# A Strassen MLP whose first products take their weight block sums from VectorE, with the tiles moved to other byte offsets

## The chip, the cores and the metric

The kernel runs on one core of one Trainium2 chip. The time is device microseconds for one execution, the median of three runs.

## The reference

One layer of a decoder with 512 tokens of width 1024, everything in float32. Two mixers run side by side on the same normalised input (sliding-window attention and a gated convolution), their outputs are gated, added and projected, and an MLP with a squared ReLU follows:

```python
u = rms_norm(x, norm_mix_g)
proj = u @ w_in                       # q, k, v, two convolution inputs, two gates
attn = sliding_window_attention(...) @ w_attn_o
conv = conformer_conv(...)           # ends in a product with w_conv_out
merged = jax.nn.sigmoid(gate_attn) * attn + jax.nn.sigmoid(gate_conv) * conv
x = x + merged @ w_out
hmid = jnp.square(jax.nn.relu(rms_norm(x, norm_mlp_g) @ w_ff1))   # 1024 -> 4096
x = x + hmid @ w_ff2                                              # 4096 -> 1024
```

## The kernel before, in words

Each float32 matrix is split into a high and a low part, each in a rounded format that TensorE multiplies at full rate, and a product is three matmuls: high by high, high by low, low by high. ScalarE (ACT) casts the high part; VectorE (DVE), or GpSimd (POOL) in some places, subtracts it from the whole to get the low part.

The program is written as a list of events, `at(pos, fn, ...)`, that is sorted by position before anything is issued. One unit of position is roughly 1.4 us of TensorE work. Each engine runs its instructions in that order, and so do the DMA queues of SP (plain loads) and POOL (loads that add to what is in the buffer). So a late instruction holds all that stands behind it on its engine or queue.

The stages are: projections, attention and convolution up to 313 us; the attention output product `ps_wo` (313 to 362 us); the convolution output product `ps_wc` (362 to 407); the product with `w_out` and the second norm (position `W0`, 407 to 453); and the MLP (position `M0 = W0 + 32`, 453.6 to 782.9).

The MLP works on four parts of the hidden width, each of 1024. A part is two phases of 28 units: an even phase is the first product (FF1: 512 x 1024 by 1024 x 1024, with `w_ff1`), an odd phase the second (FF2, with `w_ff2`). A phase is a Winograd form of Strassen's scheme with one level: seven products of half-size blocks, 4 units each, instead of eight. They run in `ORDER`: 1, 7, 6, 2, 5, 4, 3 (in phase 0: 1, 2, 7, 6, 5, 4, 3). In FF1 the weights stand in TensorE and the normalised `x` (tiles `xE`, `xO`, `xS`) streams by in 256 columns; in FF2 the activations (`aE`, `aO`, `aS`) stand and the weights stream by in 512 columns.

Of a phase's weight blocks b11, b12, b21, b22 the products need: 1: b11; 5: b11 + b12; 7: b12 + b22; 6: b11 + b12 + b22; 4: all four; 2: b21; 3: b22. A sum lies in a raw buffer of 128 x 2048 floats (two halves, `h` = 0 and 1, of 512 KB). For each half `piece_hi` (L1105, ACT) casts it to `pieceh` and `piece_lo` (L1108, DVE) subtracts to `piecel`; there are four buffers of pieces, so piece n waits until product half n - 4 has been run. `products` issues the matmuls (L1133 in FF1, L1138 in FF2).

The sums are made by the transfers: `fetch` (L1090, SP) loads a block, and `fetch_add` (L1094, POOL) loads another block with an add into the same buffer, after the pieces have read it:

```python
    BUF = {1: 0, 5: 0, 7: 1, 6: 1, 4: 1, 2: 2, 3: 2}
                if prod == 1:
                    at(d, fetch_add, ph, 0, 0, 1, h)
                elif prod == 7:
                    at(d, fetch_add, ph, 1, 0, 0, h)
                elif prod == 6:
                    at(d, fetch_add, ph, 1, 1, 0, h)
```

There are three raw buffers (`raw_b`, `raw_q0`, `raw_q1`). So each of the eight phases moves 8 MB: four plain blocks and four added ones. The results of FF1's products are combined by `c_copy`, `c_add`, `relu`, `square_of`; `operands` then makes from them the sums and splits for FF2 (`op_sum`, `op_hi`, `op_lo`). FF2's results are added to the residual rows by `row_add` (L1143).

Every tile has a byte offset in a partition's memory. The pools behind the small pool `sm` begin 192 bytes beyond a multiple of 256, those before it (`wp`, `keep`) on a multiple.

Of the kernel before, what the change touches and what calls it, by code (L numbers as in the profile page):

```python
# [17 lines left out]
P = 128  # L18
# [34 lines left out]
def tile_hybrid_block(  # L53
# [34 lines left out]
    sm.tile([P, LEAD // 4], F32, name="even", bufs=1)  # L88
# [370 lines left out]
    def split_lo(u):  # L459
        ge.tensor_tensor(out=pieces[u][1], in0=piece_of(u), in1=pieces[u][0].bitcast(F32), op=ALU.subtract)  # L460
# [197 lines left out]
    last_of = {wout[2]: b + 6.5, wout[3]: b + 12.5}  # L658
# [353 lines left out]
    def wout_split(ch, m, eng):  # L1012
        ks, raw = slice(2 * m, 2 * m + 2), raws[ch][:, 2 * (m % 2):2 * (m % 2) + 2, :]
        se.copy(tl["wouth"][:, ks, :], raw)
        eng.tensor_tensor(out=tl["woutl"][:, ks, :], in0=raw, in1=tl["wouth"][:, ks, :].bitcast(F32),
                          op=ALU.subtract)
# [31 lines left out]
    for m, p in enumerate((1.5, 6, 9.5, 12)):  # L1048
        at(W0 + p, wout_split, wout_late[m // 2], m, ge)
    at(W0 + 8, lambda: se.activation(roots[:, 0:1], epsc, AF.Sqrt))  # L1050
    for t in range(NT):
        at(W0 + 16.1 + 0.6 * t, lambda t=t: residual(t, 0, tl["acc"][t]))
        at(W0 + 16.6 + 0.6 * t, residual_square, t, 0)
# [6 lines left out]
        for half in range(2):  # L1060
            late = (0.8, 0.2, 0, 0)[t]
# [16 lines left out]
    BUF = {1: 0, 5: 0, 7: 1, 6: 1, 4: 1, 2: 2, 3: 2}  # L1078
# [17 lines left out]
    def open_mlp():  # L1096
        for n in range(2):
            tl["raw"].append(wp.tile([P, 4, S], F32, name=f"raw_q{n}", tag="raw", bufs=2))

    def open_pieces():  # L1100
        for n in "hl":
            tl["p" + n] += [wp.tile([P, 2, S], F32R, name=f"piece{n}{i}", tag="w" + n) for i in range(3)]
# [277 lines left out]
```

## Time and profile before

| | before |
|---|---|
| median of 3 runs | 788.52 us (787.55 to 788.69) |
| profiled execution | 788.5 us, span 786.7 us |
| granted clock of TensorE, mean | 0.997 |
| moved by DMA | 113.21 MB |
| on POOL's queue (adding transfers) | 33.56 MB |
| DMA in the MLP | 0.63 to 0.93 of the engines' time in each phase |

In the profile, PE is TensorE, PEld its weight loads. A row of a group of instructions gives the line, engine, operation, output <- inputs, shape and count; then the busy time in us and the mean of one in ns; then the idle time of the engine just ahead of them and what ended most of it. A row of the chain gives the time, the duration in us, what it was, and how many instructions. A row of waits gives who waited for whom: us in total, times, longest. A `DMA` row is a transfer, `raw_q` and `raw_b` being the raw buffers. Rows of the timeline give start, duration, engine, line, operation, count, and in brackets the wait ahead of it.

### The profile page before, as it was taken

The numbers are of one execution on the slowest core, as the hardware profiler recorded it, in microseconds if no ns is written. First come the engines' busy times: TensorE is split into PE (matmuls) and PEld (weight loads), VectorE is DVE, ScalarE is ACT, GpSimd is POOL, SyncE is SP. The second block draws the span as 40 slices with busy tenths as digits, with TensorE's granted clock in tenths as the row PEclk, the third lists the DMA queues.
The fourth block names the chain that finished last, engine by engine and source line by source line (L and its number), as shares of the span: only waits on it lengthen the run. The fifth ranks groups of instructions, "written<-read, shape, count | busy, mean of one in ns | idle before, by whom it ended". The sixth has DMA issues, their size and how long they took to land.

```text
span 786.7 us, 11648 instructions
## 1 busy us (share of the span) xinstructions
PE 766.4 (97%) x4464; PEld 668.5 (85%) x4464; DVE 566.0 (72%) x888; ACT 438.6 (56%) x696; POOL 332.1 (42%) x253
## 2 busy tenths in 40 slices
PE   8999999999999999999999998899999999999998
PEld 7989989898888888788888898779997899789976
DVE  5467978898888878975433577694679558875785
ACT  5445457766576665455335466652766367535851
POOL 4444978958565655334357012213131313131310
PEclk9999999999999999999999999999999999999999
DMA  8351041214141132522337637989898999899982
GB/s 272 105 173 54 1 161 54 82 54 135 53 132 58 54 107 68 201 84 77 107 130 234 145 55 183 192 208 216 218 199 202 212 229 194 194 213 207 219 167 107
DMA packets 74029, 113.21 MB, mean 144 GB/s; under 512 B 4004, under 2 KB 36820, under 8 KB 73974
## 3 DMA queue, kind: packets, MB, share of 16 engines
q1 hardware_dynamic: 56566, 78.91, 30.7%
q0 software_dynamic: 17408, 33.56, 24.2%
q8 instruction: 35, 0.57, 0.3%
q14 instruction: 20, 0.16, 0.1%
HBM read 110.33 MB, written 2.12 MB: 143 GB/s over the span
## 4 chain that ended last, share of the span: by engine, by line
PE 59%; DMA 13%; issue 10%; DVE 8%; POOL 6%; ACT 3%; POOLq 0%; SPq 0%; ACTq 0%; DVEq 0%
DMA raw_q<-in_w_ff_dram 12%; DVE piecel L1108 4%; PE ps_x L1133 3%; POOL raw_b L1094 2%; POOL raw_q L1094 2%; PE ps_ta L492 2%; PE ps_wc L492 2%; PE ps_wc L493 2%; PE ps_wc L494 2%; PE ps_ta L494 2%; PE ps_wo L196 2%; PE ps_wo L198 2%; PE ps_ta L493 2%; PE ps_wo L197 2%; PE ps_g L492 2%
## 5 line engine op out<-in xcount | busy, mean ns | idle before, releaser
L1094 POOL DMA_DIRECT2D raw_q<-in_w_ff_dram x48 | 58.8, 1226 | 222.4 <-DMA raw_q<-in_w_ff_dram 139.9
L794 DVE SCALAR_TENSOR_TENSOR cv<-h,wcol,cv 128x512 f32<-128x512 f32 x208 | 147.5, 747 | 0.5
L1108 DVE TENSOR_TENSOR piecel<-raw_q,pieceh 128x1024 fp32r<-128x1024 f32 x80 | 97.1, 1221 | 57.0 <-ACT pieceh L1105 56.9
L1105 ACT CAST pieceh<-raw_q 128x1024 fp32r<-128x1024 f32 x80 | 82.6, 1048 | 70.9 <-DMA raw_q<-in_w_ff_dram 51.5
L1108 DVE TENSOR_TENSOR piecel<-raw_b,pieceh 128x1024 fp32r<-128x1024 f32 x32 | 41.2, 1291 | 29.0 <-ACT pieceh L1105 29.0
L1133 PE MATMUL ps_x<-xSh,pieceh 128*128 128x256 f32 x192 | 54.3, 283 | 2.5 <-ACT c L1152 2.2
L1133 PE MATMUL ps_x<-xSh,piecel 128*128 128x256 f32 x192 | 54.5, 284 | 1.4 <-DVE piecel L1108 1.3
L1133 PE MATMUL ps_x<-xSl,pieceh 128*128 128x256 f32 x192 | 54.1, 282 | 0.0
L1138 PE MATMUL ps_z<-piecel,aSh 128*128 128x512 f32 x96 | 38.4, 400 | 5.4 <-DVE piecel L1108 5.4
L1105 ACT CAST pieceh<-raw_b 128x1024 fp32r<-128x1024 f32 x32 | 33.2, 1046 | 11.6 <-PE ps_y L1138 10.1
L703 ACT ACTIVATE s<-s,negm 128x257 f32<-128x257 f32 (+1 forms) x64 | 30.4, 478 | 16.2 <-DVE negm L695 16.2
L1133 PEld LDWEIGHTS ps_x<-xSh,pieceh 128*128 128x128 f32 x192 | 36.8, 191 | 2.9 <-ACT c L1152 2.4
L1138 PE MATMUL ps_z<-pieceh,aSh 128*128 128x512 f32 x96 | 37.5, 391 | 1.7 <-ACT pieceh L1105 1.7
L1133 PEld LDWEIGHTS ps_x<-xSh,piecel 128*128 128x128 f32 x192 | 36.4, 190 | 2.2 <-DVE piecel L1108 2.2
L1138 PE MATMUL ps_z<-pieceh,aSl 128*128 128x512 f32 x96 | 37.5, 391 | 0.0
L786 POOL TENSOR_TENSOR side<-side,tap 128x512 f32<-128x512 f32 x24 | 31.1, 1297 | 13.6 <-ACT tap L785 13.6
L196 PE MATMUL ps_q<-wh_q,uTh 128*128 128x256 f32 x128 | 36.6, 286 | 0.0
L1133 PEld LDWEIGHTS ps_x<-xSl,pieceh 128*128 128x128 f32 x192 | 36.4, 189 | 0.0
L727 DVE TENSOR_TENSOR pTl<-ptp,pTh 128x512 fp32r<-128x512 f32 x28 | 19.3, 690 | 23.7 <-ACT pTh L723 23.6
L198 PE MATMUL ps_q<-wh_q,uTl 128*128 128x256 f32 x128 | 36.2, 283 | 0.0
L197 PE MATMUL ps_q<-wl_q,uTh 128*128 128x256 f32 x128 | 36.2, 282 | 0.0
L1094 POOL DMA_DIRECT2D raw_b<-in_w_ff_dram x16 | 19.6, 1242 | 32.9 <-DVE piecel L1108 25.5
(325 smaller groups left out, 2600.8 us busy)
## 6 DMA issues: line engine op xcount, KB each, us to landing
raw_q<-in_w_ff_dram SPq DMA_DIRECT2D x48, 512.0 KB, 6.3
raw_q<-in_w_ff_dram POOLq DMA_DIRECT2D x48, 512.0 KB, 7.7
raw_b<-in_w_ff_dram SPq DMA_DIRECT2D x16, 512.0 KB, 8.0
raw_b<-in_w_ff_dram POOLq DMA_DIRECT2D x16, 512.0 KB, 8.8
x<-in_x_dram SPq DMA_DIRECT2D x8, 512.0 KB, 4.6
raw_g<-in_w_in_dram SPq DMA_DIRECT2D x8, 512.0 KB, 4.5
raw_a<-in_w_in_dram SPq DMA_DIRECT2D x8, 512.0 KB, 3.5
raw_q<-in_w_in_dram SPq DMA_DIRECT2D x8, 512.0 KB, 5.2
```

What stands on the lines that cost most here:

```text
L196: pe.matmul(ps, ah, wh, start=first, stop=False)
L197: pe.matmul(ps, ah, wl, start=False, stop=False)
L198: pe.matmul(ps, al, wh, start=False, stop=last)
L492: pe.matmul(ps, wh[:, k, :], ah(k), start=(k == 0), stop=False)
L493: pe.matmul(ps, wh[:, k, :], al(k), start=False, stop=False)
L494: pe.matmul(ps, wl[:, k, :], ah(k), start=False, stop=(k == KD - 1))
L794: ve.scalar_tensor_tensor(out=cps[ct], in0=src, scalar=w, in1=cps[ct], op0=ALU.mult, op1=ALU.add)
L1094: ge.dma_start(tl["raw"][buf][:, ks, :], block(ph, i, j)[:, ks, :], accum_op=ALU.add)
L1105: se.copy(tl["ph"][n % 4], tl["raw"][buf][:, 2 * h:2 * h + 2, :])
L1108: ve.tensor_tensor(out=tl["pl"][n % 4], in0=tl["raw"][buf][:, 2 * h:2 * h + 2, :], in1=tl["ph"][n % 4].bitcast(F32), op=ALU.subtract)
L1133: pe.matmul(o, b[:, c, w], a[:, k, :], start=(first and c + q + i == 0), stop=(k == 3 and i == 2), skip_group_check=True)
L1138: pe.matmul(acc, a[:, k, w], b[:, c, :], start=(first and c + i == 0), stop=(k == 3 and i == 2), skip_group_check=True)
```

## The change

*Block sums.* In FF1 phases the four blocks are loaded plainly into four raw buffers (`block0` to `block3`, whose roles `homes` rotates), and `block_sum` on DVE makes the sums in place: q1 = b11 + b12, q3 = b12 + b22, q2 = b11 + b12 + b22, q4 = that + b21, each in two halves. In phase 0 the last of these is still an adding transfer. FF2 phases keep the adding transfers, with other buffers: the sum for product 7 is loaded and added during the FF1 phase before (earlier than it was), the blocks of the next FF1 phase are loaded during FF2. So FF1 phases move 4 MB instead of 8.

*Order.* Pieces for product 6 go 2.5 units earlier in FF1, those for product 7 0.95 to 1.05 units in FF2 (`s`); first activation operands `P1`, `P2` and the later `x` operands move by 0.5 to 3.6 units. Some subtractions (`split_lo` for the second `w_out` chunk, the four `wout_lo`) move from POOL to DVE. In the `w_out` stage the buffers of blocks and pieces are opened one by one.

*Places.* The tile `even` is 64 bytes longer, a tile `shift` of 192 bytes is put in, and the order of tiles in the `ff` pool is changed. Then the FF2 operands and all four piece buffers begin on multiples of 256 bytes; `xE`, `xO`, `xS` stay 192 beyond one.

The diff, cut to its core:

```diff
-    sm.tile([P, LEAD // 4], F32, name="even", bufs=1)
+    sm.tile([P, LEAD // 4 + 16], F32, name="even", bufs=1)
...
-        ge.tensor_tensor(out=pieces[u][1], in0=piece_of(u), in1=pieces[u][0].bitcast(F32), op=ALU.subtract)
+        eng = ve if u in wout_uses[2:] else ge
+        eng.tensor_tensor(out=pieces[u][1], in0=piece_of(u), in1=pieces[u][0].bitcast(F32), op=ALU.subtract)
...
-        tl["raw"] = [pool.tile([P, 4, S], F32, name="raw_b")]
+        tl["raw"] = [pool.tile([P, 4, S], F32, name=f"block{i}") for i in range(2)]
...
+        gmlp = tl["gmlp"] = pool.tile([P, D], F32, name="gmlp", tag="aEh")
+        tl["fsq"] = pool.tile([P, 2, S], F32, name="fsq", tag="aEl")
+        pool.tile([P, 48], F32, name="shift")
+        for n in "hl":
+            tl["wout" + n] = pool.tile([P, KD, S], F32R, name=f"wout1{n}", tag="xS" + n)
...
+    def wout_hi(m):
+        se.copy(tl["wouth"][:, 2 * m:2 * m + 2, :], raws[wout_late[m // 2]][:, 2 * (m % 2):2 * (m % 2) + 2, :])
+
+    def wout_lo(m):
+        ks = slice(2 * m, 2 * m + 2)
+        ve.tensor_tensor(out=tl["woutl"][:, ks, :], in0=raws[wout_late[m // 2]][:, 2 * (m % 2):2 * (m % 2) + 2, :],
+                         in1=tl["wouth"][:, ks, :].bitcast(F32), op=ALU.subtract)
...
-    for m, p in enumerate((1.5, 6, 9.5, 12)):
-        at(W0 + p, wout_split, wout_late[m // 2], m, ge)
+    for m, p in enumerate((1.5, 2.5, 9.2, 10.2)):
+        at(W0 + p, wout_hi, m)
+        at(W0 + p + 0.75, wout_lo, m)
...
-    BUF = {1: 0, 5: 0, 7: 1, 6: 1, 4: 1, 2: 2, 3: 2}
+
+    def homes(ph):
+
+
+        w, x, y, z = 0, 1, 2, 3
+        for _ in range(ph // 2):
+            w, x, y, z = y, w, z, x
+        return (w, x, y, z) if ph % 2 == 0 else (w, z, x, x)
+
+    def home(ph, prod):
+        return homes(ph)[{1: 0, 5: 0, 7: 1, 6: 1, 4: 1, 3: 2, 2: 3}[prod]]
...
+    def block_sum(out, a, b, h):
+        o, a, b = (tl["raw"][i][:, 2 * h:2 * h + 2, :] for i in (out, a, b))
+        ve.tensor_tensor(out=o, in0=a, in1=b, op=ALU.add)
...
-    at(W0 + 15, open_mlp)
-    at(W0 + 14.1, open_pieces)
+    at(W0 + 3.5, open_block)
+    at(W0 + 11.2, open_block)
+    at(W0 + 8.1, open_pieces, 1)
+    at(W0 + 12.1, open_pieces, 1)
+    at(W0 + 16.1, open_pieces, 1)
     at(M0 - 0.5, open_banks)
     at(M0 - 0.8, open_x)
     at(M0 + 10, open_a, "E")
-    at(M0 + 20, open_a, "O")
+    at(M0 + 26, open_a, "O")
     at(M0 + 20, open_a, "S")
     operands("x", {"P1": M0 - 3.4, "P2": M0 - 1.7, "S3": M0 + 4.6, "P7": M0 + 5.1, "S2": M0 + 6.6,
-                   "P6": M0 + 7.3, "S1": M0 + 9, "P5": M0 + 11, "P4": M0 + 13, "S4": M0 + 15, "P3": M0 + 17})
+                   "P6": M0 + 7.3, "S1": M0 + 10, "P5": M0 + 11.5, "P4": M0 + 16.6, "S4": M0 + 18.6, "P3": M0 + 19.6})
     for h in range(2):
-        at(W0 + 1 + h, fetch, 0, 0, 0, 0, h)
-        at(W0 + 15.2 + h, fetch, 0, 1, 0, 1, h)
-        at(W0 + 20 + h, fetch_add, 0, 1, 1, 1, h)
-        at(W0 + 15.4 + h, fetch, 0, 2, 1, 0, h)
+        at(W0 + 1 + 0.1 * h, fetch, 0, 0, 0, 0, h)
+        at(W0 + 1.3 + 0.1 * h, fetch, 0, 1, 0, 1, h)
+        at(W0 + 4.9 + 0.1 * h, fetch, 0, 2, 1, 1, h)
+        at(W0 + 11.3 + 0.1 * h, fetch, 0, 3, 1, 0, h)
     for ph in range(PHASES):
         m = M0 + 28 * ph
         order = ORDER[ph]
         ff1 = ph % 2 == 0
+        h11, ht, h22, h21 = homes(ph)
+        if ff1:
+            for h in range(2):
+                if ph:
+                    q1, q3, q2, q4 = m - 4.3 + 2 * h, m - 3.4 + 2 * h, m - 1.0 + 2 * h, m + 8.8 + 1.2 * h
+                else:
+                    q1, q3, q2, q4 = W0 + 7.3 + 4.6 * h, W0 + 18 + 0.9 * h, m + 5.2 + 1.7 * h, m + 10.2 + 0.9 * h
+                at(q1, block_sum, h11, h11, ht, h)
+                at(q3, block_sum, ht, ht, h22, h)
+                at(q2, block_sum, ht, h11, h22, h)
+                if ph:
+                    at(q4, block_sum, ht, ht, h21, h)
+                else:
+                    at(m + 7.4 + 2 * h, fetch_add, ph, ht, 1, 0, h)
+                at(q4 + 0.1, fetch, ph + 1, h21, 0, 1, h)
+                at(q4 + 5, fetch_add, ph + 1, h21, 1, 1, h)
+        elif ph + 1 < PHASES:
+            for h in range(2):
+                at(m + 7 + h, fetch, ph + 1, homes(ph - 1)[2], 0, 0, h)
         for j, prod in enumerate(order):
             p = m + 4 * j
             for h in range(2):
                 n = 2 * (7 * ph + j) + h
-                s = p - (3.4 if prod == 6 else 5.9) + 2 * h
+                s, lo = p - 5.9 + 2 * h, 0.75
                 if ph == 0 and j < 2:
-                    s = (W0 + 14.2, W0 + 15.2, W0 + 18.6, W0 + 19.4)[n]
-                at(s, piece_hi, n, BUF[prod], h)
-                at(s + 0.75, piece_lo, n, BUF[prod], h)
+                    s, lo = ((W0 + 5.6, 0.75), (W0 + 8.2, 0.75), (W0 + 21.8, 1.1), (W0 + 22.6, 4.5))[n]
+                elif not ff1 and prod == 7:
+                    s = m - 2.95 + 3 * h
+                elif not ff1 and prod == 6:
+                    s = p - 3.4 + 2 * h
+                at(s, piece_hi, n, home(ph, prod), h)
+                at(s + lo, piece_lo, n, home(ph, prod), h)
                 for t in range(2):
                     at(p + 2 * h + t, products, ph, prod, n, h, t)
                 d = s + 0.9
-                more = ph + 1 < PHASES
-                if prod == 1:
-                    at(d, fetch_add, ph, 0, 0, 1, h)
+                if ff1:
+                    if prod == 5:
+                        at(d, fetch, ph + 1, h11, 0, 0, h)
+                    elif prod == 4:
+                        at(d, fetch, ph + 1, ht, 1, 0, h)
+                elif prod == 1:
+                    at(d, fetch_add, ph, h11, 0, 1, h)
                 elif prod == 7:
-                    at(d, fetch_add, ph, 1, 0, 0, h)
+                    at(d, fetch_add, ph, ht, 0, 0, h)
                 elif prod == 6:
-                    at(d, fetch_add, ph, 1, 1, 0, h)
+                    at(d, fetch_add, ph, ht, 1, 0, h)
                 elif prod == 2:
-                    at(d, fetch, ph, 2, 1, 1, h)
-                elif prod == 5 and more:
-                    at(d, fetch, ph + 1, 0, 0, 0, h)
-                elif prod == 4 and more:
-                    at(d, fetch, ph + 1, 1, 0, 1, h)
-                    at(d + 4.5, fetch_add, ph + 1, 1, 1, 1, h)
-                elif prod == 3 and more:
-                    at(d, fetch, ph + 1, 2, 1, 0, h)
+                    at(d, fetch, ph, h21, 1, 1, h)
+                elif ph + 1 < PHASES:
+                    at(d, fetch, ph + 1, home(ph, prod), *{5: (0, 1), 4: (1, 1), 3: (1, 0)}[prod], h)
             for t in range(2):
                 e = p + 3.1 + t
                 if ff1:
...
                     at(e, row_add, ph, half_t, half_n, prod, t, minus, store)
             if ff1 and prod in (2, 5, 4):
                 i, scale = {2: (0, 1.0), 5: (3, -1.0), 4: (2, 1.0)}[prod]
-                at(p + 4.9, relu, i, scale)
-                at(p + 5.5, square_of, i)
+                late = 7.6 if ph == 0 and prod == 2 else 0
+                at(p + 4.9 + late, relu, i, scale)
+                at(p + 5.5 + late, square_of, i)
             elif ff1 and prod == 3:
                 at(p + 4.8, square_of, 1)
         if ff1:
             e = {prod: m + 4 * j + 4 for j, prod in enumerate(order)}
-            operands("a", {"P1": m + 17.6, "S3": e[4] + 2.2, "P7": e[4] + 2.9, "S2": e[4] + 4.4, "P6": e[4] + 5.1,
-                           "P2": e[3] + 6.5, "S1": e[3] + 9.5, "P5": e[3] + 10.3, "P4": e[3] + 13.2,
+            operands("a", {"P1": m + 18.2, "S3": e[4] + 2.2, "P7": e[4] + 2.9, "S2": e[4] + 4.4, "P6": e[4] + 5.1,
+                           "P2": e[3] + 7.5, "S1": e[3] + 9.5, "P5": e[3] + 10.3, "P4": e[3] + 13.2,
                            "S4": e[3] + 16, "P3": e[3] + 17})
```

More of the change, by code (lines that the diff above doesn't have):

```diff
@@ L657, in tile_hybrid_block @@
     wout_late = wout[2:]
-    last_of = {wout[2]: b + 6.5, wout[3]: b + 12.5}
+    last_of = {}
     for u, (ch, j, _, b0, b1) in enumerate(uses):
@@ L961, in open_tail @@
         tl["pool"] = pool
-        tl["raw"] = [pool.tile([P, 4, S], F32, name="raw_b")]
+        tl["raw"] = [pool.tile([P, 4, S], F32, name=f"block{i}") for i in range(2)]
         for n in "hl":
             tl["p" + n] = [pool.tile([P, 2, S], F32R, name=f"piece{n}")]
-            tl["wout" + n] = pool.tile([P, KD, S], F32R, name=f"wout1{n}", tag="xS" + n)
         tl["u2"] = pool.tile([P, 2, D], F32, name="u2", tag="aOh")
@@ L969, in open_tail @@
         tl["ca"] = [pool.tile([P, 4, 256], F32, name=f"c{i}") for i in range(4)]
+        gmlp = tl["gmlp"] = pool.tile([P, D], F32, name="gmlp", tag="aEh")
[3 more added lines that the diff above has]
+            tl["wout" + n] = pool.tile([P, KD, S], F32R, name=f"wout1{n}", tag="xS" + n)
         tl["xE"] = [pool.tile([P, 4, 256], F32R, name=f"xE{n}") for n in "hl"]
         tl["xO"] = [pool.tile([P, 4, S], F32R, name=f"xO{n}") for n in "hl"]
-        gmlp = tl["gmlp"] = pool.tile([P, D], F32, name="gmlp", tag="aEh")
-        tl["fsq"] = pool.tile([P, 2, S], F32, name="fsq", tag="aEl")
         tl["ssm"] = whole_lines(pool, P, NT * 2, "ssm").rearrange("p (t h) -> p t h", h=2)
@@ L1010, in wout_second @@
             wout_mm(tl["acc", t], k, t, tl["wouth"][:, k, :], tl["woutl"][:, k, :])
[L1012 to L1016, printed above, removed]
+    def wout_hi(m):
[4 more added lines that the diff above has]
+                         in1=tl["wouth"][:, ks, :].bitcast(F32), op=ALU.subtract)
     def residual(t, half, acc):
@@ L1047, in tile_hybrid_block @@
             at(W0 + 4 * i + 2 * j, wout_first, u, i, j)
-    for m, p in enumerate((1.5, 6, 9.5, 12)):
-        at(W0 + p, wout_split, wout_late[m // 2], m, ge)
+    for m, p in enumerate((1.5, 2.5, 9.2, 10.2)):
+        at(W0 + p, wout_hi, m)
+        at(W0 + p + 0.75, wout_lo, m)
     at(W0 + 8, lambda: se.activation(roots[:, 0:1], epsc, AF.Sqrt))
     for t in range(NT):
-        at(W0 + 16.1 + 0.6 * t, lambda t=t: residual(t, 0, tl["acc"][t]))
-        at(W0 + 16.6 + 0.6 * t, residual_square, t, 0)
+        at(W0 + 16.1 + 0.5 * t, lambda t=t: residual(t, 0, tl["acc"][t]))
+        at(W0 + 16.6 + 0.5 * t, residual_square, t, 0)
         e = W0 + 20 + 4 * t
@@ L1060, in tile_hybrid_block @@
         for half in range(2):
-            late = (0.8, 0.2, 0, 0)[t]
+            late = (1.2, 0.2, 0, 0)[t]
             at(e + 3.6 + late + 0.2 * half, x2_trans, t, half)
@@ L1094, in fetch_add, with open_block, open_pieces @@
         ge.dma_start(tl["raw"][buf][:, ks, :], block(ph, i, j)[:, ks, :], accum_op=ALU.add)
[L1096 to L1100, printed above, removed]
+    def open_block():
+        n = len(tl["raw"])
+        tl["raw"].append(wp.tile([P, 4, S], F32, name=f"block{n}", tag="raw", bufs=2))
+    def open_pieces(more):
         for n in "hl":
-            tl["p" + n] += [wp.tile([P, 2, S], F32R, name=f"piece{n}{i}", tag="w" + n) for i in range(3)]
+            for _ in range(more):
+                i = len(tl["p" + n])
+                tl["p" + n].append(wp.tile([P, 2, S], F32R, name=f"piece{n}{i}", tag="w" + n))
+    def block_sum(out, a, b, h):
+        o, a, b = (tl["raw"][i][:, 2 * h:2 * h + 2, :] for i in (out, a, b))
+        ve.tensor_tensor(out=o, in0=a, in1=b, op=ALU.add)
     def piece_hi(n, buf, h):
```

## The prediction

> **What bounds the kernel now.** I read the page first, then the MLP by stage: what TensorE (PE) waits for from 453 us on, a table of windows cut at the eight MLP phases (an even one is a first product FF1, an odd one a second product FF2), and the chain of work that ended last.
>
> ```profile
> span 786.7 us, 11648 instructions
> PE 766.4 (97%) x4464; PEld 668.5 (85%) x4464; DVE 566.0 (72%) x888; ACT 438.6 (56%) x696; POOL 332.1 (42%) x253
> L1094 POOL DMA_DIRECT2D raw_q<-in_w_ff_dram x48 | 58.8, 1226 | 222.4 <-DMA raw_q<-in_w_ff_dram 139.9
> L1108 DVE TENSOR_TENSOR piecel<-raw_q,pieceh 128x1024 fp32r<-128x1024 f32 x80 | 97.1, 1221 | 57.0 <-ACT pieceh L1105 56.9
> ```
> ```profile
> PE ps_z L1138 <- DVE piecel L1108: 5.4, 6, 1.0
> PE ps_x L1133 <- ACT c L1152: 2.2, 1, 2.2
> PE ps_z L1138 <- ACT pieceh L1105: 1.7, 1, 1.7
> PE ps_x L1133 <- DVE piecel L1108: 1.3, 3, 0.8
> ```
> ```profile
> 453.60:496.80 43.20, 41.03 (x347) 40.83 (x346) 32.53 (x37) 28.49 (x36) 8.46 (x7) 1.00 0.63 134
> 496.80:539.60 42.80, 39.37 (x170) 31.42 (x169) 35.40 (x37) 24.19 (x26) 10.47 (x9) 1.00 0.90 203
> 539.60:581.00 41.40, 40.30 (x337) 39.86 (x336) 23.60 (x24) 24.43 (x28) 10.14 (x9) 1.00 0.92 211
> 581.00:621.00 40.00, 39.05 (x170) 31.44 (x169) 35.18 (x37) 22.02 (x24) 9.68 (x8) 1.00 0.91 205
> 621.00:661.30 40.30, 40.05 (x337) 39.83 (x336) 22.93 (x24) 24.52 (x27) 9.69 (x8) 1.00 0.92 211
> 661.30:702.30 41.00, 39.24 (x171) 31.46 (x170) 34.90 (x37) 22.04 (x23) 9.68 (x8) 1.00 0.90 204
> 702.30:742.60 40.30, 39.95 (x337) 39.54 (x336) 22.96 (x25) 24.50 (x27) 9.69 (x8) 1.00 0.93 213
> 742.60:782.90 40.30, 39.26 (x170) 31.28 (x169) 32.33 (x36) 18.88 (x20) 4.84 (x4) 1.00 0.64 146
> ```
> ```profile
> 453.90 5.71 PE ps_x L1133 x48
> 460.48 5.66 PE ps_z L1133 x48
> ...
> 766.45 5.45 PE ps_z L1138 x24
> 771.90 5.50 PE ps_y L1138 x24
> ```
>
> PE is the bound: 766.4 of the 786.7 us, at a granted clock of 1.00 in every phase. So only two things can shorten the kernel: the waits of PE, and the time of one matmul. In the windows (start and end, length, then busy time of PE, weight loads, DVE, ACT, POOL; clock; DMA share; GB/s) the length is set against seven undisturbed products: FF1 7 x 5.69 = 39.8 us (mean of 5.71 and 5.66), FF2 7 x 5.48 = 38.4 (of 5.45 and 5.50). What is over is waiting: FF1 phases 2, 4, 6: 1.6 + 0.5 + 0.5 = 2.6; FF2 phases 1, 3, 5, 7: 4.4 + 1.6 + 2.6 + 1.9 = 10.5. Phase 0 has 3.4 over, part of it eleven more PE instructions (x347); its wait is the single 2.2 us for the copy L1152. That makes 15.3 us.
>
> In FF2, and in FF1 phases 2, 4 and 6, the waits are for pieces (L1105, L1108), at product 6, the third in order. Its block sum is made in place by POOL's accumulating transfer, and that cannot start before the pieces of product 7 have read the buffer:
>
> ```profile
> 582.97 1.21 POOL L1094 DMA_DIRECT2D raw_q<-in_w_ff_dram  x1 [2.22 <-DVE piecel L1108]
> 586.57 1.20 POOL L1094 DMA_DIRECT2D raw_q<-in_w_ff_dram  x1 [2.39 <-DVE piecel L1108]
> ```
> ```profile
> 582.97 7.07 DMA raw_q<-in_w_ff_dram
> 590.11 1.06 ACT pieceh L1105
> ...
> 595.21 1.22 DVE piecel L1108
> ...
> 745.04 6.62 DMA raw_q<-in_w_ff_dram
> ```
>
> A loop of piece, 1.2 us of issue, 7 us to landing (this includes the issue), cast, subtraction.
>
> **FF1 phases 2, 4, 6: accumulation off, sums on.** Removed: eight accumulating issues on POOL and 4 of 8 MB per phase, with the 7 us in the loop. Added: eight vector adds of 128x1024. The nearest row is another vector operation of that size with two SBUF operands:
>
> ```profile
> L1186 DVE SCALAR_TENSOR_TENSOR c<-c,c 128x1024 f32<-128x1024 f32 x8 | 9.8, 1221 | 0.1
> L1143 DVE TENSOR_TENSOR x<-x,ps_z 128x512 f32<-128x512 f32 x32 | 20.5, 680 | 4.1 <-PE ps_z L1138 4.1
> 591.00:617.00 26.00, 25.05 (x109) 20.00 (x108) 25.60 (x28) 15.12 (x16) 5.97 (x5) 1.00 0.80 196
> 614.22 1.22 DVE L1108 TENSOR_TENSOR piecel<-raw_b,pieceh 128x1024 fp32r<-128x1024 f32 x1
> ```
>
> 8 x 1.22 = 9.8 us per phase, and FF1 has room (DVE 23 of 40). The tight place is the junction with the FF2 phase before it: from 591 to 617 DVE is busy 25.60 of 26.0, and six of the eight sums come right behind. Written out from 614.2, where DVE starts the first piece of phase 4: two pieces of product 1, four sums and the first piece of product 7 are 7 x 1.22 = 8.5, two residual adds between them 1.4; so piece (7, first half) is done at 624.1. PE needs it at 621.0 + 5.7 = 626.7: 2.6 us to spare. Two more steps each of a sum and a piece (2.4) give 626.5 against 629.5, and 629.0 against 632.4. The sums are hidden by product 1, and the 2.6 us of waits go. If a sum took 0.4 us more, this cover would be used up (six sums, 2.6 us). Gain 2.6; ends: 0, and 2.6.
>
> On the queues: SP issues sixteen half fetches per pair of phases as before (six in FF1, ten in FF2), each behind the last reader of its buffer, so on SP a late one holds the ones behind it. The blocks of an FF1 phase are all issued during the FF2 phase before it (from 7 units behind its start to product 3), each at least 9 units, some 13 us, ahead of the sum that reads it, against some 7 us to landing; this covers them. POOL keeps two accumulations per FF1 phase, for product 7 of the next FF2 phase, issued 5 units (7 us) behind the fetch that they add to; behind them on POOL nothing is queued until FF2's first.
>
> **FF2: order changed, accumulation stays.** The sum for product 7 is added some 6 units earlier in the phase before (unit 13.8 instead of 19.6); PE does not wait for it now, and it stays hidden behind products 5 and 4. The pieces of product 7 move from 1.9 units (one is about 1.4 us) ahead of the phase to 2.95, the second half to 0.05 behind its start. So the first half's accumulation starts some 1.3 us earlier; in phase 3 its piece was about 1.1 us late, and that goes. The second half gains nothing: DVE must first finish the activation sum that now stands ahead of it, and I have its piece ending at 587.2, against 584.94 + 1.22 before:
>
> ```profile
> 584.94 1.22 DVE L1108 TENSOR_TENSOR piecel<-raw_q,pieceh 128x1024 fp32r<-128x1024 f32 x1
> ```
>
> Issue at 587.5, landing 6.6 to 7.1 later, cast 1.06, subtraction 1.22: 596.4 to 596.9. PE would want it at 581.0 + 2 x 5.48 + 2.74 = 594.7, or later by what it waited before. That is 1.7 to 2.2 in phase 3; DVE being less behind in the other phases (its sum is 34.9 and 32.3 there against 35.2) I take 1.3 for each, 5.2 of the 10.5. Gain 5.3; ends: nothing (all 10.5 stay) and 10.5. Where this wait goes, product 2 is next in order; its block b21 is loaded plainly in the phase before, so no wait takes the place.
>
> The later places of P1 and P2 among the activation operands, of the x operands, and the later opening of aO cost nothing while DVE keeps ahead of product 1 of FF2, which starts with P1; DVE's FF1 share (23 of 40) with 9.8 more leaves 7 us. If it were late, it would be in the first product and by a step, 1.2 us.
>
> **Phase 0 and the stage before.** Its wait is ACT standing in order at a cast that waits for an accumulating transfer:
>
> ```profile
> 478.07 1.04 ACT L1105 CAST pieceh<-raw_q 128x1024 fp32r<-128x1024 f32 x1 [1.20 <-DMA raw_q<-in_w_ff_dram]
> ```
>
> This 1.20 goes; the rest of the 2.2 is the casts and copies themselves, 1.0 that stay. Gain 1.2; ends 0 and 2.2. The six vector subtractions that leave POOL (two chunk splits, four of the second output chunk) cost DVE 6 x 1.22 = 7.3 from 407 to 453, where it is far from full; what covers them is the 45 us of output products. The block fetches of phase 0 go out in the first 12 units of that stage instead of up to unit 21, three sums on DVE replace the accumulations there, and the pieces' buffers open one by one as the output chunks leave theirs; only the fourth block is still accumulated, at unit 7 to 9 of the phase, for product 4, the sixth.
>
> **Placement.** FF2 operands, and most stationary pieces, come to multiples of 256 bytes. The chain has the same product with the two operands placed unlike (aTh, 192 beyond a multiple, against weights on one) and alike (aTl):
>
> ```profile
> 313.88 7.46 PE ps_wo L472 x32
> 321.35 3.65 PE ps_wo L476 x16
> L196 PE MATMUL ps_wo<-wout1h,mTh 128*128 128x512 f32 x32 | 12.8, 400 | 0.0
> L196 PE MATMUL ps_wo<-wh_wout,mTh 128*128 128x512 f32 x32 | 12.5, 389 | 0.0
> L311 PE MATMUL ps_v<-vw,uTh 128*128 128x256 f32 x32 | 7.5, 277 | 0.0
> L196 PE MATMUL ps_q<-wh_q,uTh 128*128 128x256 f32 x128 | 36.6, 286 | 0.0
> ```
>
> 7.46/32 = 233 ns unlike, 3.65/16 = 228 alike: 5 ns. The two output chunks agree in sign (400 unlike, 389 alike). Some 320 matmuls of the two mixer output stages become alike (1.6 us), and 240 of FF2's 672 (192 whose activations, 48 whose piece alone lies off the multiple; 1.2). At 256 columns the sign is the other way (277 unlike, 286 alike). FF1's pieces in the one buffer that was alike become unlike: a quarter of 1344 at half the 5.71 to 5.66 difference read as 2 ns each, 0.7 gain; the 192 k and v matmuls become alike, at most 192 x 9 ns = 1.7 loss, I take half, 0.9. Net gain 2.6; ends 0 and 4.5. *A rule against it:* the Trainium skill ("TensorE: Matmul & The Clock Gate", Part 2: What happens when you issue a matmul) says that PE has two independent SBUF read ports, so that loading the next weights does not take read bandwidth from the running matmul; by that the placement of one against the other would give nothing, and the sum 779.4. The rows differ by 5 to 11 ns, so here I go by the rows.
>
> **Sum.** 2.6 + 5.3 + 1.2 + 2.6 = 11.7 us off the profiled execution, which took 788.5 us (span 786.7, 1.8 around it), the median of the runs being 788.52. **Forecast 776.8 us.**
>
> **The rivals.**
> *A, slower: DVE becomes the bound at the three FF2 to FF1 junctions.* One pair of subtractions ran at half speed beside POOL arithmetic:
>
> ```profile
> 424.28 4.61 DVE L1108 TENSOR_TENSOR piecel<-raw_b,pieceh 128x1024 fp32r<-128x1024 f32 x2 [14.38 <-ACT pieceh L1105]
> 421.83 4.84 POOL L1015 TENSOR_TENSOR wout1l<-raw_wout,wout1h 128x1024 fp32r<-128x1024 f32 x2 [2.10 <-ACT wout1h L1014]
> ```
>
> At 2.3 instead of 1.22, nine operations of a junction are 9.7 us longer, 7.1 beyond the 2.6 to spare, three times 21: 776.8 + 21 = 798. It decides from 6.5 us per junction, 0.7 each. Against it: POOL only issues transfers in the MLP, and beside its issues 80 subtractions average 1221 ns. The Trainium skill ("SBUF — State Buffer", SBUF: two separate sides) has a vector operation with two SBUF inputs and a GpSimd operation reading SBUF exclude each other; the pair above agrees, but no row shows it for POOL's issues.
> *B, FF2 waits as before:* the loop through POOL is kept, and its landing rather than its start may decide: 776.8 + 5.3 = 782.1.
> *C, FF2 waits vanish:* half the traffic in FF1 and earlier sums make landings shorter: 776.8 - 5.2 = 771.6. Against: 6.62 us stands in phase 7, where the DMA share is lowest (0.64).
> *D, placement gives nothing:* 779.4.
> *E, no effect:* the waits move to other pieces, since each still needs a cast and a subtraction in order: about 788.
>
> **How the numbers follow.** Forecast 0.37, B 0.20, C 0.13, D 0.14, E 0.05, A 0.11. The range 771 to 786 leaves out A, E and little of B. 0.2% (1.6 us) is about what a measurement of this kernel can tell from no change. Faster 0.84; same 0.05 (E); slower 0.11 (A).
>
> **What would show it.** Right: FF1 phases 2, 4, 6 of 39.3 to 40 us with no wait for a piece; FF2 phases of about 39.4, their wait at product 6's second half; phase 0 about 42; mixer output products at 228 ns. Wrong: DVE sums above 1.6 us each, a wait at product 7 or 6 of an FF1 phase, or FF2 phases still above 40.5.

## The result, and the profile after

The changed kernel takes **775.3 us** (median of four runs, 772.98 to 776.15) against 788.61 for the kernel before: ratio 0.9829, 95% interval 0.9805 to 0.9852. On another chip it gave 774.63 us and a ratio of 0.9807 (0.9783 to 0.9831). The forecast was 776.8. The profiled execution took 776.15 us, span 774.4.

The page of the changed kernel:

```profile
span 774.4 us, 11619 instructions
PE 761.1 (98%) x4464; PEld 668.6 (86%) x4464; DVE 604.7 (78%) x924; ACT 438.5 (57%) x696; POOL 281.3 (36%) x217
L1124 DVE TENSOR_TENSOR block<-block,block 128x1024 f32<-128x1024 f32 x30 | 36.6, 1221 | 0.8 <-DMA block<-in_w_ff_dram 0.4
```

The sums are there: 30 on DVE at 1.221 us, as estimated; POOL is 51 us less busy, DVE 39 us more. What PE waits for in the MLP:

```profile
PE ps_z L1160 <- DVE piecel L1130: 1.7, 3, 0.8
PE ps_z L1160 <- ACT pieceh L1127: 0.5, 1, 0.5
PE ps_x L1155 <- ACT c L1174: 0.4, 1, 0.4
```

The eight phases in the same kind of windows, cut where the phases now begin:

```profile
453.80:495.10 41.30, 40.76 (x347) 40.17 (x346) 34.88 (x39) 28.75 (x37) 6.26 (x5) 1.00 0.54 128
495.10:536.20 41.10, 39.10 (x171) 31.39 (x170) 37.07 (x39) 23.62 (x26) 6.04 (x5) 1.00 0.80 179
536.20:575.70 39.50, 39.50 (x337) 39.50 (x336) 31.40 (x32) 24.68 (x28) 4.84 (x4) 1.00 0.55 144
575.70:614.20 38.50, 38.42 (x171) 31.51 (x170) 35.48 (x37) 21.63 (x23) 4.84 (x4) 1.00 0.78 181
614.20:653.70 39.50, 39.50 (x337) 39.50 (x336) 31.43 (x32) 24.73 (x28) 4.84 (x4) 1.00 0.56 144
653.70:692.30 38.60, 38.38 (x170) 31.50 (x170) 35.43 (x37) 21.68 (x23) 4.84 (x4) 1.00 0.77 181
692.30:731.90 39.60, 39.60 (x337) 39.56 (x337) 31.52 (x32) 24.80 (x28) 4.84 (x4) 1.00 0.47 116
731.90:770.50 38.60, 38.56 (x170) 31.29 (x168) 31.91 (x34) 18.90 (x20) 4.82 (x4) 1.00 0.62 141
```

And products on the chain that ended last (start, duration):

```profile
314.62 7.25 PE ps_wo L473 x32
...
541.98 5.65 PE ps_y L1155 x48
...
598.02 5.44 PE ps_z L1160 x24
603.46 5.44 PE ps_y L1160 x24
```

How to read this: in phases 2, 4 and 6 PE is busy in the whole window (39.50 of 39.50), so not one wait is left in those FF1 phases. An undisturbed product has one length per kind from phase 1 on, 5.65 and 5.44, where before there were two or three. Seven times 5.44 is 38.1, so the FF2 phases wait 3.0, 0.4, 0.5 and 0.5 us, 4.4 in all. (The view of waits has 2.2 for the same: it leaves out what passes while a started matmul still counts as busy. A wait of a phase is here always its length less seven undisturbed products, unless the view is named.) Phase 0 has lost 1.9 us. Together the MLP went from 329.3 us (453.60 to 782.90 in the windows) to 316.7.

The span fell by 12.3 us, all of it in the MLP; the stages ahead of it seem to have gained nothing. But the mixer product now runs at 7.25/32 = 227 ns a matmul, as expected. What took it back is a fall of the granted clock. In these windows (clock: third number from the end) it is 0.78 for 6 us and then still 0.98:

```profile
313.80:337.00 23.20, 23.20 (x102) 18.67 (x100) 21.02 (x28) 9.94 (x14) 9.60 (x5) 1.00 0.54 182
337.00:343.00 6.00, 5.79 (x29) 4.91 (x28) 3.81 (x14) 1.04 (x1) 3.44 (x2) 0.78 0.51 175
343.00:362.00 19.00, 19.00 (x87) 15.79 (x87) 14.31 (x24) 15.17 (x23) 4.82 (x2) 0.98 0.17 56
```

That is about 1.7 us lost. One of the four runs had a mean clock of 1.000 and a span of 771.2; the three with 0.994 to 0.995 had 773.3 to 774.4. So such falls make most of the spread between these four. In the kernel before they do not: beside the repeated run below, its runs at 0.995 to 0.996 took 787.51 to 794.12 us.

### The profile page after: what moved, and what is told of

The parts are those of the page before. It is cut to its first block, busy times and chain, and to the rows that moved or that the text cites. A ratio compares the mean times of both kernels' runs of the same rounds, so it can differ in the third digit from the quotient of the medians.

```text
span 774.4 us, 11619 instructions
## 1 busy us (share of the span) xinstructions
PE 761.1 (98%) x4464; PEld 668.6 (86%) x4464; DVE 604.7 (78%) x924; ACT 438.5 (57%) x696; POOL 281.3 (36%) x217
## 4 chain that ended last, share of the span: by engine, by line
PE 81%; DVE 6%; DMA 4%; ACT 3%; issue 3%; POOL 2%; SPq 0%; DVEq 0%; ACTq 0%; POOLq 0%
PE ps_x L1155 9%; PE ps_z L1160 8%; PE ps_y L1155 4%; PE ps_y L1160 4%; DMA block<-in_w_ff_dram 3%; PE ps_x L1160 3%; PE ps_z L1155 2%; PE ps_ta L493 2%; PE ps_ta L495 2%; PE ps_wo L197 2%; PE ps_wo L198 2%; PE ps_wo L196 2%; PE ps_g L493 2%; PE ps_ta L494 2%; PE ps_wc L495 2%
## 5 line engine op out<-in xcount | busy, mean ns | idle before, releaser
L1130 DVE TENSOR_TENSOR piecel<-block,pieceh 128x1024 fp32r<-128x1024 f32 x112 | 136.0, 1220 | 36.1 <-ACT pieceh L1127 36.0
L1127 ACT CAST pieceh<-block 128x1024 fp32r<-128x1024 f32 x112 | 115.7, 1047 | 73.6 <-DVE block L1124 21.4
L1110 POOL DMA_DIRECT2D block<-in_w_ff_dram x34 | 41.3, 1245 | 298.8 <-DVE piecel L1130 175.2
L1124 DVE TENSOR_TENSOR block<-block,block 128x1024 f32<-128x1024 f32 x30 | 36.6, 1221 | 0.8 <-DMA block<-in_w_ff_dram 0.4
L1194 ACT CAST aSh<-c 128x1024 fp32r<-128x1024 f32 x16 | 16.8, 1048 | 28.8 <-DVE c L1208 13.2
L713 POOL TENSOR_TENSOR s<-s,r 128x1024 f32<-128x1024 f32 (+1 forms) x16 | 26.9, 1682 | 14.7 <-DVE r L708 14.7
```

The costliest lines, as they stand in the source:

```text
L1110: ge.dma_start(tl["raw"][buf][:, ks, :], block(ph, i, j)[:, ks, :], accum_op=ALU.add)
L1124: ve.tensor_tensor(out=o, in0=a, in1=b, op=ALU.add)
L1127: se.copy(tl["ph"][n % 4], tl["raw"][buf][:, 2 * h:2 * h + 2, :])
L1130: ve.tensor_tensor(out=tl["pl"][n % 4], in0=tl["raw"][buf][:, 2 * h:2 * h + 2, :], in1=tl["ph"][n % 4].bitcast(F32), op=ALU.subtract)
```

## The experiments

Each stands beside runs of the kernel before on the same chip; ratios are to these.

**The changed kernel again** (no edit).

> The changed kernel once more, beside the other three of this group, so that they have it on the same chip. Theory: 775.3 us again, FF1 products of 5.65 us without a wait, FF2 products of 5.44. Rival: the granted clock, which fell to 0.78 for 6 us at 337 us in its first profile, decides a few us between executions; then executions at a clock of 1.00 are at 773 and those at 0.995 at 775 to 776.

774.63 us, ratio 0.9807 (0.9783 to 0.9831). FF1 products 5.65 without a wait, FF2 5.44, as in the first profile; this time the clock fell twice in the first 20 us and not at 340. The two runs at a clock of 1.000 took 773.1 and 773.4 us, the two at 0.995 775.8 and 776.1: the clock decides some 2.5 us between executions.

**The places alone, on the kernel before.**

```diff
-    sm.tile([P, LEAD // 4], F32, name="even", bufs=1)
+    sm.tile([P, LEAD // 4 + 16], F32, name="even", bufs=1)
...
+        pool.tile([P, 48], F32, name="shift")
```
and the tiles of the `ff` pool in the order of the changed kernel.

> The kernel before with the new places of the tiles alone (the sums still by adding transfers, the old order). Theory: unlike or alike places set the time of a matmul, whatever the sums do: FF2 products 5.44 us instead of 5.45 to 5.60, FF1 products 5.65 instead of 5.66 to 5.71, mixer output products 228 ns a matmul instead of 233; together 0.8 (FF1) + 1.7 (FF2) + 1.9 (mixers) - 0.9 (k, v) = 3.5 us, so 785 us if all of it reaches the end. Rival 1: the waits at product 6 hang on the transfers and take part of it back: 786 to 787. Rival 2: places do nothing, 788.5.

789.22 us, ratio 0.9984 (0.9967 to 1.0002): no gain that can be told. Yet the products did get shorter: all FF2 products without a wait are 5.44, and the MLP begins at 452.2 instead of 453.6. The waits took it back:

```profile
PE ps_z L1140 <- DVE piecel L1110: 5.0, 6, 1.0
PE ps_z L1140 <- ACT pieceh L1107: 3.9, 3, 2.6
PE ps_x L1135 <- ACT c L1154: 2.1, 1, 2.1
PE ps_x L1135 <- DVE piecel L1110: 2.0, 3, 0.8
```

In FF2 (`ps_z`, L1140) they are 8.9 us by this view against 7.1 before: the loop through POOL ends when it ends, and a faster PE arrives earlier and waits. That is rival 1, with two falls of the clock inside the MLP (about 1.7 us each) on top.

**The change without the places.** The same tile edits undone on the changed kernel.

> The changed kernel with the old places of the tiles (sums on VectorE and the new order stay). Theory: the waits go as they went in the changed kernel (15 us to about 5), the products keep 5.66 to 5.71 and 5.45 to 5.60: 788.5 - 10 = 778.5 us. Rival: if placement does nothing, the time of the changed kernel, 775.3.

776.59 us, ratio 0.9838 (0.9815 to 0.986), so the sums and the order carry most of the gain, the places 2.0 us by the medians, with intervals that overlap. Its FF2 phase 3:

```profile
576.80:615.30 38.50, 38.50 (x170) 31.60 (x169) 35.64 (x37) 21.98 (x23) 4.82 (x4) 1.00 0.78 181
```

There is no wait in it: with the old places seven undisturbed FF2 products take 38.5 us, not 38.1. And it is as long as the changed kernel's, 38.50, which has faster products and waits 0.4. So in FF2 the gain of the places is lost to a wait here too; it shows in FF1 (0.2 us a phase) and ahead of the MLP (1.4 us: 454.7 against 453.3 in the repeated changed kernel, whose first 20 us had the same falls of the clock).

**FF2's products in another order**, to give product 6 more time.

```diff
-    ORDER = [(1, 2, 7, 6, 5, 4, 3)] + [(1, 7, 6, 2, 5, 4, 3)] * (PHASES - 1)
+    ORDER = [(1, 2, 7, 6, 5, 4, 3)] + [(1, 7, 2, 6, 5, 4, 3), (1, 7, 6, 2, 5, 4, 3)] * PARTS
-            operands("a", {... "P2": e[3] + 7.5,
+            operands("a", {... "P2": e[3] + 4.5,
```

> The changed kernel with FF2's products in the order 1, 7, 2, 6, 5, 4, 3, and the operand P2 three units earlier, so that the adding transfer for product 6 has one product (5.44 us) more. Theory: FF2's 4.1 us of waits (2.9 in phase 1, 0.3 to 0.5 in the others) are the landing of that transfer: they go, all FF2 phases are 38.1 us, 771.3 us. Rival: the wait moves to product 2, whose operand VectorE must make 3 units earlier in its fullest stretch: about 775 or more.

786.16 us, ratio 0.9952 (0.9932 to 0.9972): 11.5 us worse than the changed kernel. The rival holds, and more strongly than it was put:

```profile
PE ps_z L1160 <- DVE x L1165: 6.8, 4, 1.7
PE ps_x L1160 <- DVE aOl L1198: 3.0, 4, 2.3
```

No wait for a piece is left, but PE now waits in all four FF2 phases for DVE, for the operand of product 2 (aO) and for the residual adds (L1165) that must empty the accumulator. DVE is full there (busy 16.5 of the 16.8 us from 585.0 to 601.8, in phase 3); what is moved ahead for one product is taken from another.

**Each sum twice.**

```diff
         ve.tensor_tensor(out=o, in0=a, in1=b, op=ALU.add)
+        ve.tensor_tensor(out=o, in0=o, in1=o, op=ALU.max)
```

> The changed kernel with a second VectorE instruction of the same size (both inputs from SBUF, a maximum of the sum with itself, so the value stays) behind each block sum. It measures how far the junction from FF2 to FF1 is from VectorE being the bound. Six of the eight sums of an FF1 phase stand at the junction: 6 x 1.14 = 6.8 us more there. Theory (2.6 us to spare, as worked out from the trace of before): a wait of about 4.2 us at products 7 and 6 in each of phases 2, 4, 6, 12.6 us in all, 787 us. Rival 1: more to spare, because PE got faster by less than VectorE got freer: under 2 us a junction, 775 to 781. Rival 2: sums beside POOL's transfers stretch when doubled, above 790.

797.74 us, ratio 1.01 (1.0079 to 1.0121), slower than the kernel before. In the FF1 phases PE now waits for the pieces behind the sums:

```profile
PE ps_y L1156 <- DVE piecel L1131: 11.0, 6, 2.9
```
```profile
538.40:547.20 8.80, 5.96 (x51) 5.76 (x49) 8.64 (x8) 2.10 (x2) 0.00 (x0) 1.00 0.00 0
547.30:552.00 4.70, 4.56 (x24) 4.36 (x24) 4.67 (x5) 2.02 (x3) 0.00 (x0) 0.64 0.01 3
```
```profile
561.24 5.44 PE ps_z L1156 x48
```

Phases 2, 4, 6 are 4.9, 4.9 and 5.6 us longer than in the changed kernel, where 4.2 were forecast for each. In phase 2 PE reads the first low piece of product 6 at 555.73, 17.4 us into the phase; in the changed kernel it does so at 11.5. Of these 5.9 us four products at 5.44 (third fence) gave back 0.84. The clock fell in between (0.64 over 4.7 us right behind the first wait, second row), but that cost nothing of its own: PE waits another 0.65 us for that low piece, so DVE sets the end and a faster PE would only have waited longer.

So less was to spare than the 2.6 us worked out. The changed kernel's own trace shows it, in phase 4: the low piece of product 7's second half, and the matmul that reads it first.

```profile
620.53 1.22 DVE L1130 TENSOR_TENSOR piecel<-block,pieceh 128x1024 fp32r<-128x1024 f32 x1
622.89 0.28 PE L1155 MATMUL ps_y<-xSh,piecel 128*128 128x256 f32 x1
```

That is 1.1 us (621.75 against 622.89); for product 7's first half it is 1.9, for product 6's first half 1.6. The rest of the 23 us lies in FF2 (4.7) and phase 0 (2.5). So 787 was too low at the junctions (15.5 us for 12.6) and left the other phases out; rival 2's stretched sums are not it, since both kinds keep their size (1220 and 1225 ns).

**x on multiples of 256 too.**

```diff
-        pool.tile([P, 48], F32, name="shift")
```

> The changed kernel without the shift tile, so that xE, xO and xS also begin on multiples of 256 bytes, like the pieces. Theory (at 256 columns alike is slower, as in the first piece buffer before): FF1 products 5.75 us instead of 5.65, 4 x 7 x 0.1 = 2.8 us more, 777.4. Rival: what matters is a multiple of 256 for every operand; FF1 products stay or become shorter, 775 or less.

777.18 us, ratio 0.9847 (0.9827 to 0.9867), and FF1 products as the theory has them, 5.76 for 5.65 (40.3 us a phase for 39.6):

```profile
552.64 5.76 PE ps_z L1154 x48
558.40 5.76 PE ps_x L1154 x48
```

**Phase 0's last sum on DVE.**

```diff
-                if ph:
-                    at(q4, block_sum, ht, ht, h21, h)
-                else:
-                    at(m + 7.4 + 2 * h, fetch_add, ph, ht, 1, 0, h)
+                at(q4, block_sum, ht, ht, h21, h)
```

> The changed kernel with the last adding transfer of FF1, that of b21 in phase 0, also made a VectorE sum. In the changed kernel its second half landed 13.6 us after issue, and phase 1 waits 2.9 us at product 6. Theory: that late landing holds POOL's queue and with it the sum for product 7 of phase 1; the wait of phase 1 falls to the 0.3 to 0.5 of the other FF2 phases, 772.2 us. Rival: the wait of phase 1 is the loop through POOL for product 6 alone, and stays: 774.6, or 775 to 776 with two more vector operations in phase 0.

774.55 us, ratio 0.9808 (0.9789 to 0.9827): by the time, the same as the changed kernel. In the trace phase 1's wait falls from 3 to 2.2 us, not to 0.4; the late landing was a small part of it.

**The same, and product 7's second piece in FF2 one unit earlier.**

```diff
-                    s = m - 2.95 + 3 * h
+                    s = m - 2.95 + 2 * h
```

> As the kernel ph0_dve, and in FF2 the second half of product 7's piece one unit earlier, ahead of the activation sum S2. Theory: the waits of 0.3 to 0.5 in phases 3, 5, 7 stand at product 6's second half because its adding transfer starts late behind that piece; they go (1.2 us), 771.0 us. Rival: S2 and P6, now behind it, come late and product 6 waits for its operand: 772 or more.

772.07 us, ratio 0.9779 (0.9763 to 0.9796): 2.5 us less than ph0_dve on the same chip. Phase 1 and phase 3:

```profile
492.70:532.10 39.40, 38.56 (x170) 31.42 (x169) 36.71 (x38) 23.10 (x25) 5.95 (x5) 1.00 0.81 187
571.70:609.80 38.10, 38.10 (x171) 31.55 (x170) 35.82 (x38) 22.17 (x23) 4.84 (x4) 1.00 0.79 183
```

Phases 3, 5 and 7 wait for nothing, phase 1 still 1.3 us. So what the changed kernel still waited for in phases 3, 5 and 7 was product 6's second half behind a late piece of product 7, as the theory says.

**Product 7's pieces in FF2 where they were before.**

```diff
                 elif not ff1 and prod == 7:
-                    s = m - 2.95 + 3 * h
+                    s = m - 1.9 + 2 * h
```

> The changed kernel with the pieces of product 7 in FF2 where they were before (1.9 units ahead of the phase and 0.1 behind its start, instead of 2.95 ahead and 0.05 behind). It tells what shortened FF2's waits. Theory (the earlier start of the loop through POOL): the first half's wait comes back in phases 3, 5, 7, some 1.1 to 1.5 us each beside the 0.3 to 0.5 that are there, 778.5 us. Rival (half the traffic in FF1 makes the landings shorter): the waits stay at 0.3 to 0.5 each, 774.6.

772.98 us, ratio 0.9775 (0.9742 to 0.9808). Neither: the waits do not come back, and next to nothing of the 0.3 to 0.5 is left (phase 1 still waits 1.8). Phase 3, and the two accumulations for product 6 on POOL there, then the same two of the changed kernel:

```profile
573.80:612.00 38.20, 38.20 (x171) 31.65 (x170) 36.40 (x38) 21.83 (x23) 4.84 (x4) 1.00 0.80 183
```
```profile
575.17 1.21 POOL L1110 DMA_DIRECT2D block<-in_w_ff_dram  x1 [2.24 <-DVE piecel L1130]
578.78 1.22 POOL L1110 DMA_DIRECT2D block<-in_w_ff_dram  x1 [2.40 <-DVE piecel L1130]
```
```profile
575.81 1.20 POOL L1110 DMA_DIRECT2D block<-in_w_ff_dram  x1 [0.95 <-DVE piecel L1130]
581.68 1.22 POOL L1110 DMA_DIRECT2D block<-in_w_ff_dram  x1 [4.67 <-DVE piecel L1130]
```

DVE of the changed kernel there, and then the landing times of the adding transfers issued from 573 to 583 us, first in p7_late, then in the changed kernel:

```profile
574.17 1.23 DVE L1130 TENSOR_TENSOR piecel<-block,pieceh 128x1024 fp32r<-128x1024 f32 x1 [0.93 <-ACT pieceh L1127]
...
577.65 1.23 DVE L1198 TENSOR_TENSOR aSl<-c,aSh 128x1024 fp32r<-128x1024 f32 x1 [1.12 <-ACT aSh L1194]
```
```profile
DMA to landing us min/median/max: 5.6/5.8/6.0
```
```profile
DMA to landing us min/median/max: 5.7/7.0/7.4
```

From the phase's start, the halves are issued at 1.4 and 5.0 us with the late places (573.81 the start) and at 0.1 and 5.9 with the early ones (575.73). The early first piece leaves DVE idle twice for ACT (0.93 ahead of that piece, 1.12 ahead of the operand), and the second half, which decides, goes out 1 us later, though its own place differs by only 0.05 units. The first half lands at about the same point, 7.3 and 7.5 us into the phase, because its transfer is the longest of either row, and shorter when issued later (6.0 against 7.4 us). In phases 5 and 7 it does land later with the late places, by 1.6 and 0.4 us, but in neither kernel does PE wait for the first half in phases 3, 5 and 7.

What shortened these waits against the kernel before stands in its trace and in the changed kernel's. In phase 3 of the kernel before, nearly all of the wait is for product 6's second half. ACT and DVE there, then DVE of the changed kernel at the same point:

```profile
592.02 1.04 ACT L1172 CAST aOh<-c 128x1024 fp32r<-128x1024 f32 x1
593.48 0.68 DVE L1143 TENSOR_TENSOR x<-x,ps_y 128x512 f32<-128x512 f32 x1
594.07 1.22 DVE L1176 TENSOR_TENSOR aOl<-c,aOh 128x1024 fp32r<-128x1024 f32 x1
595.21 1.22 DVE L1108 TENSOR_TENSOR piecel<-raw_q,pieceh 128x1024 fp32r<-128x1024 f32 x1
```
```profile
588.52 1.23 DVE L1130 TENSOR_TENSOR piecel<-block,pieceh 128x1024 fp32r<-128x1024 f32 x1 [1.18 <-ACT pieceh L1127]
590.26 1.22 DVE L1198 TENSOR_TENSOR aOl<-c,aOh 128x1024 fp32r<-128x1024 f32 x1
```

Before, the transfer issued at 586.57 landed 11.5 us into the phase, but the operand of product 2 (`aOh`, `aOl`) stood ahead of the piece on both engines, and the piece was done at 15.4. In the changed kernel the transfer lands at 11.7, no earlier, and DVE stands idle until the cast is there (1.18 us); the piece is done at 14.0. The operand now comes behind it, because `P2` was moved from 6.5 to 7.5. From landing to finished piece it is 3.9 us in phases 3, 5 and 7 before, and 2.3 in those of the changed kernel; place_only, which keeps `P2` at 6.5, has 3.4 to 3.9, and this run, with 7.5, 2.3 to 2.7. No run moves `P2` alone.

**The x tiles 64 and 128 bytes beyond a multiple** (on ph0_h1).

```diff
-        pool.tile([P, 48], F32, name="shift")
+        pool.tile([P, 16], F32, name="shift")     # x_64;  x_128: [P, 32]
```

> As ph0_h1, with the shift tile of 64 bytes instead of 192, so xE, xO, xS begin 64 beyond a multiple of 256. FF1 has been seen at three paces: 5.76 us a product (x alike), 5.65 (x at 192), and 5.44 (x at 192, in some phases that began behind a wait). Theory 1: any place off the multiple gives 5.65, 772.1 us. Theory 2: two read streams meet in the same bank or not by their distance; then this distance gives another pace, 5.44 at best (4 x 7 x 0.21 = 5.9 us less, 766) or 5.76 (775).

> As ph0_h1, with the shift tile of 128 bytes. Theory 1: 5.65 us a product in FF1 as with 192, 772.1 us. Theory 2: another pace, 5.44 at best (766 us) or 5.76 (775).

x_64: 771.69 us, ratio 0.9756 (0.973 to 0.9782). x_128: 775.05 us, 0.9798 (0.9772 to 0.9824). FF1 products, x_64 first:

```profile
550.03 5.65 PE ps_z L1155 x48
```
```profile
549.59 5.76 PE ps_z L1155 x48
```

Theory 1 fails for 128: at 0 and 128 bytes FF1 has 5.76, at 64 and 192 it has 5.65. The distance counts modulo 128 as far as these four go, and 64 brings nothing over 192. Why it counts is not shown.

**Both edits that helped FF2** (ph0_dve and p7_late).

> Both edits that helped FF2, together: phase 0's last sum on VectorE (ph0_dve) and the pieces of product 7 in FF2 at their places of before (p7_late). Theory: the waits add up as they stand in the two traces: none in phases 3, 5, 7, and phase 1 below the 1.7 us of p7_late because its queue on POOL is shorter; 771 to 772 us, the fastest here. Rival: phase 1 is bound by its own first transfers, as in ph0_h1 (1.3 us), and the time is that of ph0_h1, 772.1, or of p7_late, 773.

771.99 us, ratio 0.9775 (0.9755 to 0.9794). No wait in phase 3 (38.1 us); phase 1 still waits 1.2. It, ph0_h1 and x_64 cannot be told apart; all are below the changed kernel's 774.6 to 775.3. What holds phase 1 for its last 1.2 us stays open.

## Why the prediction was right, and where it was not

- *FF1: 2.6 us of waits go, hidden by product 1.* Right: no wait in phases 2, 4, 6, sums of 1.221 us. But the cover was thinner than worked out, 1.1 us at its tightest where the prediction has 2.6 to 3.4. Its list of what DVE does there has two residual adds (1.4 us); two more stand ahead of product 7's second piece, which was done 7.6 us into the phase and not 5.5.
- *Rival A.* Real but not reached. Doubled sums make DVE the bound, at the place that it names, and for 6.8 us more of work a junction grows by 4.9 to 5.6. The row behind its 2.3 us hides two sizes in a mean: one subtraction of 3.48 us, which began while a POOL subtraction was running, and one of 1.21. So one operation was held up once; it was not half speed for both. In the changed kernel 17 of the 112 piece subtractions ran beside one of POOL's issues and took 1.22 us like the others (of the sums, 1 of 30). So the exclusive lock that the Trainium skill ("SBUF — State Buffer", SBUF: two separate sides) gives for a vector operation with two SBUF inputs beside a GpSimd operation reading SBUF did not show where POOL only issues transfers.
- *FF2: 5.2 of 10.5 us stay.* The total was near (4.4 stay; the 10.5 were 9.8 by the 38.5 of no_place), but the reason was wrong, so that was luck. The step that failed is "the first half's accumulation starts some 1.3 us earlier, and that goes". It does start earlier, but in phases 3, 5 and 7 nothing waits for the first half, and p7_late, without that step, has fewer waits. (In phases 1 and 5 of the kernel before PE waited for the first half too, 3.0 and 1.1 us; that fell to 1.0 and nothing, and in p7_late to 0.8 and nothing.) The change of place in fact cost the second half 1 us. Most of the gain in phases 3, 5 and 7 came from a step that the prediction put at nothing, the later place of `P2`: it takes 1.5 us out of the way from landing to finished piece in each of phases 3, 5 and 7. The second half's transfers were also shorter (6.0, 7.2 and 6.4 us before, 5.7, 5.9 and 5.7 in the changed kernel, at a DMA share of 0.78 instead of 0.91); that half the traffic in FF1 did this is not shown, and the later issue used most of it up. The waits were also spread wrongly: 1.3 in each phase forecast, 3.0, 0.4, 0.5, 0.5 found.
- *Phase 0: 1.2.* Its length fell by 1.9 us, of which 0.3 are faster products (by place_only, 42.9 us against 43.2). So some 1.6 us of wait went (1.3 in the repeated run): of the 1.0 that was to stay, about half stayed.
- *Placement: 2.6.* The rows were read rightly (5 ns at 512 columns, the other sign at 256), and the matmuls gained more than put: ahead of the MLP 1.4 us, FF1 0.8, FF2 1.7. Wrong was to add that to the FF2 term: the faster products of FF2 only wait longer for the same transfers. Net 2.0 us by the medians on the changed kernel, nothing that can be told on the kernel before. By the Trainium skill ("TensorE: Matmul & The Clock Gate", Part 2: What happens when you issue a matmul) two independent read ports would leave no such effect, as the prediction took it; the four places of x disagree with that, 5.65 against 5.76 us.

So 11.7 us were forecast and 13.3 measured. By the traces the span fell by 12.3, and rounded that is 7.3 in FF2 (6.5 forecast, with its share of the places), 3.4 in phases 2, 4 and 6 and 1.9 in phase 0, less 0.2 ahead of the MLP, where the clock took back the 1.4 of the places. That the errors nearly cancel is luck.

## What to carry to other kernels

When a wait is for a piece, follow the piece from the transfer's landing to its end, and ask what else the two engines do ahead of it; here moving an operand by one unit was worth more than starting the transfer earlier. A wait and the speed of the waiting engine are not two terms of a sum: what makes the engine faster is paid back as waiting wherever another loop sets the end, so cost the loop first and the engine second. When an instruction is moved earlier, follow what its engine then idles for: here the earlier piece of product 7 left DVE waiting for ACT, and delayed the half that mattered. A doubled operation shows where an engine off the critical path becomes the bound; how much it has to spare is read from the time between each result and its first reader.

## What the runs showed of the hardware that was not expected

*Three paces of the same matmul.* A 48-matmul product of 256 columns took 5.76, 5.65 or 5.44 us (120, 118, 113 ns each), each for whole products. The first two go with the distance of the operands modulo 128 bytes. The third came only in products behind a wait, and mostly stayed to the end of the phase (561.24 in double_sums; products 4 and 3 of phase 0 in ph0_h1); in phase 6 of the kernel before it lasted one product. Not every wait brings it, and what decides it is open. At that pace FF1 would be 1.5 us a phase shorter.

*The falls of the clock.* They look alike in these traces: some 3.4 us at half the clock each, so 1.7 us lost. The one at 340 us in the changed kernel:

```profile
340.30:343.70 3.40, 3.40 (x10) 2.61 (x9) 2.60 (x12) 0.00 (x0) 0.34 (x1) 0.50 0.67 238
```

It has no wait of PE of 0.7 us or more in the 20 us ahead of it. Of the five falls inside the MLP, four came within 6 us behind the four longest waits there (from one matmul's start to the next 2.95 us in place_only, about 3.1 in each of double_sums' three junctions), the fifth in place_only behind two of 1.4 and 1.3 us. Waits of 2.4 us (kernel before) and 2.7 us (ff2_order) brought none. So long waits and falls go together here, but what decides a fall is open.
